# A hybrid decode layer on one core: projection operands in rows of one offset, value products two heads at a time, part of the last residual add on TensorE

## The chip, the cores and the metric

The kernel runs on one core of a Trainium2 chip. The metric is device time of one execution, in microseconds (us). The engines named below are TensorE (PE in the profile; PEld is its weight load), VectorE (DVE), ScalarE (ACT), GpSimd (POOL) and the DMA queues, of which SyncE's (SP) carries most. SBUF is the memory that the engines work from, PSUM the one that PE adds up in.

## The reference

One layer for a prompt of 1024 tokens with 16 learned meta tokens ahead of it, and for 64 sample tokens (8 sequences of 8), all in float32 with a width of 2048:

```python
h = rmsnorm(xp, norm_pre)                       # the same for xs, the sample tokens
q_a, k_a, v_a, gate_a, q_g, k_g, v_g, gate_g, z = split(h @ w_in)
log_f = log_sigmoid(z @ w_a2 + b_a) / 16
att_o = swa_prompt(q_a, k_a, v_a, sinks, rel_bias)   # 16 heads of 64, 4 of keys, window 128
gla_o, s_fin = gla_prompt(q_g, k_g, v_g, log_f)      # 4 heads, a state of 128x256 each
mixed = concat([att_o * silu(gate_a), rmsnorm(gla_o) * silu(gate_g)])
xp = xp + rmsnorm(mixed @ w_out, norm_post)
# samples: swa_sample over cached keys and values, gla_chunk from the cached state
return y_prompt, y_sample, the last 128 keys and values, states (prompt and sample)
```

## The kernel before, in words

Tokens lie along the free axis. Half A is 512 of them (16 meta and 496 of the prompt), half B 592 (528 of the prompt, 64 of the samples). The width of 2048 is 16 K-tiles of 128 partitions. The order of the work is: `in_half(A)`, all input projections of half A; `in_half(B)`, the same for half B; `out_first`, the output projection of half A; and `out_second` twice, the output projection of half B for its token columns 0 to 295 and then 296 to 591 (`last`). The weights come anew from DRAM for each of these passes.

Each float32 product is three matmuls with operands of type float32r (L377): the tokens are kept as two tiles, `hh` (rounded) and `hl` (the rest), which `split` (L192) writes, one pair for each K-tile, 16 of each; a weight block is `whi` (ACT, L341) and `wlo` (DVE, L343), made from `wraw`, 512 KB, which SP loads (L332, three buffers). `proj` (L362) adds up `whi*hh`, `whi*hl` and `wlo*hh` over 16 K-tiles in PSUM tiles `mm`. In half A a matmul has 512 columns, in half B two of 296 stand side by side, in `out_first` there is one of 496, in each pass of `out_second` one of 296. That makes 768 of 512 columns, 2112 of 496 and 5760 of 296, each with 128 rows of weights. So the `hh` and `hl` tiles are read by all 8640 of these matmuls; a tile is `[128, 592]`, 2368 bytes in each partition, and the 32 lie one behind the other in SBUF in the order in which `split` makes them.

Around the projections stand the lanes: generators (`att`, `glas`, `side`) which `proj` advances in its middle and at its end (`mid`, `end`). The scheduler keeps nearly everything in the order of the program text; `pin` makes it do so. Attention of half A and B is `attend` and `kv_tokens`; the decode's attention is `attend_ext` (L602), run twice, once for each pair of key heads: its value products (L674 to L680) multiply probabilities with new and cached values for one head, 64 columns of the array, and then for the other. `gla` (L690) is the gated linear attention.

What goes over from half A to B are the last 128 keys and values of each key pair (`kcar`, `vcar`) and the four states (`scar`), kept in SBUF tiles; POOL copies keys and values there (L493, L494) and back (L475, L1072), and the states are written and read in place (L891).

At the end the last pass has its 16 output tiles in eight slots `os_`; `finish` (L1224) computes the norm's factor `rs` from the sum of squares (a matmul with ones, L1229), multiplies each slot with it (L1248) and adds the residual `x` (L1249), both on DVE, while ACT's queue issues the stores.

Of the kernel before, what the change touches and what calls it, by code (L numbers as in the profile page):

```python
# [7 lines left out]
F32 = mybir.dt.float32  # L8
F32R = mybir.dt.float32r
# [14 lines left out]
TT = (M, M + 80)  # L24
W = max(TT)
FT_BUFS = 14

# [13 lines left out]
class Kernel:  # L41
    def __init__(self, tc, ins, outs, stack):
        self.tc = tc
        self.nc = tc.nc
        self.i = ins
        self.o = outs
        pool = lambda **kw: stack.enter_context(tc.tile_pool(**kw))
        self.const = pool(name="const", bufs=1)
        self.hp = pool(name="hp", bufs=1)
        self.wp = pool(name="wp", bufs=1)  # L50
        self.fp = pool(name="fp", bufs=1)
        self.sp_ = pool(name="sm", bufs=1)
# [35 lines left out]
    def setup_late(self):  # L88
# [11 lines left out]
        self.mix = [[self.dp.tile([P, TT[h]], F32, name=f"mix{h}_{k}") for k in range(KT)] for h in range(2)]  # L100
        self.kcar = c.tile([P, 2, P], F32, name="kcar")
        self.vcar = c.tile([P, 2, P], F32, name="vcar")
        self.scar = c.tile([P, 4, 256], F32, name="scar")
        yield
# [87 lines left out]
    def split(self, src, T, kt, scale=None, c0=0):  # L192

        nc = self.nc
        hi = self.hp.tile([P, W], F32R, name="hh", bufs=KT)
        lo = self.hp.tile([P, W], F32R, name="hl", bufs=KT)
        if scale is None:
            nc.scalar.copy(hi[:, c0:T], src[:, c0:T])
            nc.vector.tensor_tensor(lo[:, c0:T], src[:, c0:T], hi.bitcast(F32)[:, c0:T], ALU.subtract)  # L199
        else:  # L200
            nc.scalar.activation(hi[:, c0:T], src[:, c0:T], AF.Copy, scale=scale)  # L201
            nc.vector.scalar_tensor_tensor(lo[:, c0:T], src[:, c0:T], scale, hi.bitcast(F32)[:, c0:T],  # L202
                                           op0=ALU.mult, op1=ALU.subtract)
        self.hh[kt] = hi
        self.hl[kt] = lo
# [265 lines left out]
    def kv_tokens(self, H, c, kf, vT, vt, kh, kl):  # L471

        nc = self.nc
        if H.i:
            nc.gpsimd.tensor_copy(vt[:, 0, :], self.vcar[:, c, :])  # L475
            ps = self.ps()
            nc.tensor.transpose(ps[:16, :P], vT[:, M:M + 16], self.ident)
            nc.tensor.transpose(ps[:64, P:2 * P], vT[:, M + 16:M + 80], self.ident)
            nc.scalar.copy(vt[:16, 5, :], ps[:16, :P])
            nc.scalar.copy(vt[:64, 6, :], ps[:64, P:2 * P])  # L480
# [11 lines left out]
        if H.i == 0:  # L492
            nc.gpsimd.tensor_copy(self.kcar[:, c, :], kf[:, 512:640])  # L493
            nc.gpsimd.tensor_copy(self.vcar[:, c, :], vt[:, 4, :])  # L494
        else:
# [24 lines left out]
    def attend(self, H, c, g, q, gate, vt, kh, kl):  # L520
# [8 lines left out]
        if H.i == 0:  # L529
            first = self.sm([P, 2, P], "first", 1)  # L530
            nc.vector.tensor_tensor(first, bias, self.neg.unsqueeze(1).to_broadcast([P, 2, P]), ALU.add)
# [70 lines left out]
    def attend_ext(self, c, qx, gx, kf, vt):  # L602
# [66 lines left out]
        po = self.ps()  # L669
        for v in range(2):  # L670
            d = slice(64 * v, 64 * v + 64)
            sb = sbs[:, v]
            for w in range(2):
                nc.tensor.matmul(po[d, w * P:(w + 1) * P], vt[:64, 6, d], sb[:64, 256 + w * P:256 + (w + 1) * P],  # L674
                                 start=True, stop=False)
                for b in range(4):
                    sl = slice(w * P + 32 * b, w * P + 32 * b + 32)
                    nc.tensor.matmul(po[d, sl], vc[w][:, b, d], sb[:, sl], start=False, stop=(b == 3))
            nc.tensor.matmul(po[d, 256:320], vt[:, 4, d], tsb[:, v, :64], start=True, stop=False)
            nc.tensor.matmul(po[d, 256:320], vt[:16, 5, d], tsb[:16, v, 64:], start=False, stop=True)  # L680
        pov = po[:, :256].rearrange("p (b g t) -> p b g t", b=8, g=4)
# [8 lines left out]
    def gla(self, H, hd, zT, io):  # L690
# [174 lines left out]
        nc.vector.tensor_tensor(qe[:, :T], q[:, :T], qe[:, :T], ALU.mult)  # L865

        ktT = self.sm([P, 4, P], "kT", 2)
        ps = self.ps()
# [3 lines left out]
        if H.i:  # L872
# [6 lines left out]
            nc.scalar.copy(ktx[:64, 1], ps[:64, P:2 * P])  # L879
            nc.vector.tensor_tensor(ktx[64:, 1], ps[:64, P:2 * P], ktx.bitcast(F32)[:64, 1], ALU.subtract)  # L880
            st = [self.ft()[:, :512].rearrange("p (b d) -> p b d", b=2) for _ in range(4)]
            for b in range(4):
                self.pin(nc.sync.dma_start(out=st[b], in_=self.i["state"][hd][:, 2 * b:2 * b + 2]))
        yield
        S = [self.scar[:, hd, :] if H.i else None]
        for j in range(4):
# [153 lines left out]
    def in_half(self, H):  # L1040
        nc = self.nc
        kf = vt = kh = kl = qx = gx = None
        for u in range(4):
# [23 lines left out]
            if u % 2 == 0:  # L1067
# [126 lines left out]
    def out_second(self, H, cols, slots, last):  # L1194
# [29 lines left out]
        def finish():  # L1224
# [10 lines left out]
            def load(j):  # L1235
                x = self.ft()
                nc.sync.dma_start(out=two(x), in_=src[:, 2 * j:2 * j + 2, c0:c1])
                return x

            lead = 5 if last else 2  # L1240
            xs = [load(j) for j in range(lead)]
            before = []
            out = nc.scalar if last else nc.sync

            pin = self.pin if last else lambda x: x

            def norm(o, x, k):
                pin(nc.vector.tensor_tensor(o, o, rs[:, :T].unsqueeze(1).to_broadcast([P, k, T]), ALU.mult))  # L1248
                pin(nc.vector.tensor_tensor(o, o, x, ALU.add))  # L1249

            for j in range(KT // 2):
                if before:
                    out.dma_start(**before.pop())
# [3 lines left out]
                if last and j == KT // 2 - 1:  # L1257
                    for k in range(2):
                        norm(o[:, k:k + 1], x[:, k:k + 1], 1)
                        out.dma_start(out=dst[:, 2 * j + k:2 * j + k + 1, c0:c1], in_=o[:, k:k + 1])  # L1260
                    break
                norm(o, x, 2)
                before.append(dict(out=dst[:, 2 * j:2 * j + 2, c0:c1], in_=o))
                if last:
                    out.dma_start(**before.pop())
                yield
            if before:
                out.dma_start(**before.pop())

# [160 lines left out]
```

## Time and profile before

| What | Value |
|---|---|
| Time, median of 3 runs (lowest to highest) | 1728.17 us (1721.74 to 1729.71) |
| The profiled execution: time, span of the trace | 1732.93 us, 1731.2 us |
| Granted TensorE clock, mean of the span | 0.991 |
| PE busy, weight loads busy | 1698.1 us (98%), 1532.8 us (89%) |
| DVE, ACT, POOL busy | 1061.2, 740.8, 19.8 us |
| DMA | 213.71 MB, mean 123 GB/s |

The profile is of one execution, the trace of which is read below. A matmul's recorded duration is from its start to its modelled end and is longer than the step to the next one's start, since they are pipelined; what a matmul costs in a row of them is the step. A group's row gives the count behind an x, then the busy time of all and the mean of one.

### The profile page before, as it was taken

How to read it: one execution, taken by the hardware profiler on the slowest of the kernel's cores; microseconds unless marked ns; L12 is line 12 of the kernel's file. 1: busy time of each engine (PE TensorE's matmuls, PEld its weight loads, DVE VectorE, ACT ScalarE, POOL GpSimd, SP SyncE). 2: the span in 40 equal slices, each digit the busy share in tenths (PEclk: the TensorE clock that was granted, in tenths of full speed). 3: DMA queues.
4: the chain of work that ended last, by engine and by line, in shares of the span. 5: the costliest groups of instructions: out<-in, count | busy, mean ns of one | idle time of the engine just before them, and what ended most of it. 6: DMA issues, size and time to landing. Idle time of an engine off the chain costs nothing.

```text
span 1731.2 us, 30015 instructions
## 1 busy us (share of the span) xinstructions
PE 1698.1 (98%) x11836; PEld 1532.8 (89%) x11836; DVE 1061.2 (61%) x2360; ACT 740.8 (43%) x1606; POOL 19.8 (1%) x60
## 2 busy tenths in 40 slices
PE   8999999999999999999999999999999999999995
PEld 6778888888888999999999999999997788899995
DVE  6485686675756757545665566465857433675655
ACT  6354355443434535342444243343435333644442
POOL 0000000000000000000000000000000000000000
PEclk9999999999999999999999999999999999999998
DMA  6743433222234422323222232223325333686664
GB/s 232 125 129 98 134 109 117 91 87 93 94 96 157 167 83 71 103 71 97 83 81 91 94 113 65 92 84 101 97 83 192 107 98 98 235 273 210 217 208 162
DMA packets 85742, 213.71 MB, mean 123 GB/s; under 512 B 11504, under 2 KB 33936, under 8 KB 85568
## 3 DMA queue, kind: packets, MB, share of 16 engines
q1 hardware_dynamic: 82416, 204.90, 36.1%
q0 software_dynamic: 992, 4.46, 1.7%
q10 hardware_dynamic: 2192, 2.43, 0.4%
q8 instruction: 93, 1.52, 0.4%
q14 instruction: 49, 0.40, 0.1%
HBM read 186.32 MB, written 27.39 MB: 123 GB/s over the span
## 4 chain that ended last, share of the span: by engine, by line
PE 89%; DMA 5%; DVE 3%; ACT 1%; issue 1%; SPq 0%; DVEq 0%; ACTq 0%
PE mm L377 76%; PE ps L551 2%; DMA wraw<-in_win 1%; PE ps L581 1%; DMA ft<-in_xB 1%; PE ps L403 1%; PE ps L567 1%; PE ps L890 1%; PE ps L918 1%; DVE wlo L343 1%; PE ps L920 1%; DMA st<-in_xA 1%; PE ps L583 1%; PE ps L797 1%; DMA ft<-in_xA 1%
## 5 line engine op out<-in xcount | busy, mean ns | idle before, releaser
L377 PE MATMUL mm<-hh,whi 128*128 128x296 f32 (+2 forms) x2880 | 845.7, 333 | 7.0 <-ACT whi L341 5.9
L377 PE MATMUL mm<-hh,wlo 128*128 128x296 f32 (+2 forms) x2880 | 839.4, 331 | 3.8 <-DVE wlo L343 3.7
L377 PE MATMUL mm<-hl,whi 128*128 128x296 f32 (+2 forms) x2880 | 838.1, 330 | 0.3 <-DVE hl L199 0.3
L341 ACT CAST whi<-wraw 128x512 fp32r<-128x512 f32 x544 | 334.5, 619 | 777.9 <-PE mm L377 703.3
L343 DVE TENSOR_TENSOR wlo<-wraw,whi 128x512 fp32r<-128x512 f32 x544 | 369.9, 687 | 400.7 <-ACT whi L341 376.4
L377 PEld LDWEIGHTS mm<-hh,whi 128*128 128x128 f32 x2880 | 506.2, 189 | 49.7 <-ACT whi L341 6.6
L377 PEld LDWEIGHTS mm<-hh,wlo 128*128 128x128 f32 x2880 | 507.2, 189 | 44.3 <-DVE wlo L343 6.5
L377 PEld LDWEIGHTS mm<-hl,whi 128*128 128x128 f32 x2880 | 508.9, 189 | 37.6 <-issue 0.9
L431 DVE TENSOR_TENSOR ft<-mm,rs 128x592 f32<-128x592 f32 (+2 forms) x59 | 42.9, 727 | 64.4 <-PE mm L377 64.3
L515 ACT ACTIVATE st<-st,nm 128x128 f32<-128x128 f32 (+1 forms) x140 | 54.7, 392 | 51.7 <-DVE nm L509 51.6
L570 DVE TENSOR_TENSOR pT<-ps,c_sides 128x512 f32<-128x512 f32 x64 | 41.5, 682 | 0.9 <-PE ps L567 0.8
L433 DVE SCALAR_TENSOR_TENSOR ft<-mm,rs 128x592 f32<-128x592 f32 (+1 forms) x23 | 16.7, 725 | 32.2 <-PE mm L377 32.0
L764 DVE TENSOR_TENSOR ft<-ft 128x512 f32<-128x512 f32 (+2 forms) x48 | 33.3, 703 | 0.2
L812 DVE COPY_PREDICATED A<-masks,ps 32x64 f32<-32x64 uint8 x128 | 30.9, 241 | 3.0 <-PE ps L801 0.7
L551 PE MATMUL ps<-kh,qst 128*128 128x256 f32 x128 | 32.7, 290 | 0.0
L538 ACT CAST qst<-ft 64x256 fp32r<-64x256 f32 x64 | 25.9, 404 | 15.5 <-PE ps L551 12.5
L551 PE MATMUL ps<-kl,qst 128*128 128x256 f32 x128 | 31.1, 278 | 0.0
L765 ACT ACTIVATE ft<-ft 128x256 f32<-128x256 f32 (+2 forms) x48 | 20.3, 423 | 19.8 <-DVE ft L764 19.7
L539 DVE TENSOR_TENSOR qst<-ft,qst 64x256 fp32r<-64x256 f32 x64 | 26.9, 420 | 3.1 <-ACT qst L538 1.2
L202 DVE SCALAR_TENSOR_TENSOR hl<-ft,wpre,hh 128x512 fp32r<-128x512 f32 (+1 forms) x32 | 24.1, 788 | 6.7 <-ACT hh L201 6.7
L581 PE MATMUL ps<-pT,vt 128*64 128x128 f32 x256 | 27.3, 291 | 0.8 <-DVE pT L570 0.8
L555 DVE CUSTOM_DVE_ANT_0 st<-ps,bias 128x128 f32<-128x128 f32 x112 | 26.7, 283 | 0.0
(332 smaller groups left out, 1456.7 us busy)
## 6 DMA issues: line engine op xcount, KB each, us to landing
wraw<-in_win SPq DMA_DIRECT2D x174, 512.0 KB, 3.9
wraw<-in_wout SPq DMA_DIRECT2D x96, 512.0 KB, 4.0
ft<-in_xB SPq DMA_DIRECT2D x48, 296.0 KB, 4.6
ft<-mix SPq DMA_DIRECT2D x16, 296.0 KB, 5.9
ft<-in_xA SPq DMA_DIRECT2D x16, 256.0 KB, 5.8
ft<-in_state SPq DMA_DIRECT2D x16, 256.0 KB, 5.6
out_gs<-ft SPq DMA_DIRECT2D x16, 256.0 KB, 2.3
mix<-ft SPq DMA_DIRECT2D x16, 248.0 KB, 2.0
```

Of the source, the lines that this page charges most:

```text
L341: nc.scalar.copy(hi, r)
L343: nc.vector.tensor_tensor(lo, r, hi.bitcast(F32), ALU.subtract)
L377: nc.tensor.matmul(ps[:, j, :p1 - p0], w[:, k % 4, :], h[kt][:, p0:p1], start=(kt == 0 and a == 0), stop=(kt == KT - 1 and a == 2))
L431: self.nc.vector.tensor_tensor(o, src, r, ALU.mult)
L515: nc.scalar.activation(s, s, AF.Exp, bias=nm[:R, j:j + 1], accum_out=den[:R, j:j + 1])
L539: nc.vector.tensor_tensor(qs[o, v], qd, qs.bitcast(F32)[d, v], ALU.subtract)
L551: nc.tensor.matmul(ps[:, t], qs[:, v, t * P:t * P + P], k[:, v, k0:k0 + 256], start=(j == 0), stop=(j == 1))
L555: nc.vector.tensor_tensor_reduce(out=st[:, v, t], in0=ps[:, t, P:], in1=b[:, v], scale=1.0, scalar=NEG, op0=ALU.add, op1=ALU.max, accum_ou ...
L570: nc.vector.tensor_tensor(sb[:, j], pt, self.sides[:, j:j + 1].to_broadcast([P, 4, P]), ALU.mult)
L581: nc.tensor.matmul(pov, vt[:, j + 1, d], sb[:, 1, 2 * v + t], start=True, stop=alone)
L764: nc.vector.tensor_tensor(ev, bv, bv[:, :, h - 1:h].to_broadcast([P, ns, 2 * h]), ALU.subtract)
L812: nc.vector.copy_predicated(A[r, :, r].rearrange("p j (s e) -> p j s e", e=2 * h)[:, :, :, h:], mk[r, 16 * b:16 * b + 16].rearrange("p (s ...
```

## The change

There are four edits. **One**: the 32 token tiles are 640 floats wide instead of 592, 2560 bytes, and their pool is allocated first. Columns used stay the same. In each partition they began at byte 31296 before, with row after row 2368 bytes further; read as an offset within 512 bytes, the rows began at 64, 256, 448, 128, 320, 0, 192, 384 and again from 64, in the order in which the tiles are made, that is hh and hl of one K-tile and then of the next. Now the first begins at byte 16512 and all 32 at 128 within 512. **Two**: `kcar`, `vcar` and `scar` are DRAM tiles; eight stores and eight loads from SP's queue take the place of POOL's copies, the state gets a fifth buffer `S`, and `first` in `attend` takes a slot of `kx`. **Three**: in `attend_ext` the value products alternate between the two heads, with one more `yield` in between. **Four**: in the last pass, slots 0, 1, 2 and 5 get their residual added on PE, by matmuls with the identity into PSUM, and ACT copies the sum out and issues the store; slots 3, 4, 6 and 7 stay on DVE, and SP issues their stores.

```diff
+WH = 640
...
+        self.hp = pool(name="hp", bufs=1)
         self.const = pool(name="const", bufs=1)
-        self.hp = pool(name="hp", bufs=1)
...
-        self.kcar = c.tile([P, 2, P], F32, name="kcar")
-        self.vcar = c.tile([P, 2, P], F32, name="vcar")
-        self.scar = c.tile([P, 4, 256], F32, name="scar")
+        self.kcar = [self.dp.tile([P, P], F32, name=f"kcar{j}") for j in range(2)]
+        self.vcar = [self.dp.tile([P, P], F32, name=f"vcar{j}") for j in range(2)]
+        self.scar = [self.dp.tile([P, 256], F32, name=f"scar{j}") for j in range(4)]
...
-        hi = self.hp.tile([P, W], F32R, name="hh", bufs=KT)
-        lo = self.hp.tile([P, W], F32R, name="hl", bufs=KT)
+        hi = self.hp.tile([P, WH], F32R, name="hh", bufs=KT)
+        lo = self.hp.tile([P, WH], F32R, name="hl", bufs=KT)
...
-            nc.gpsimd.tensor_copy(vt[:, 0, :], self.vcar[:, c, :])
+            nc.sync.dma_start(out=vt[:, 0, :], in_=self.vcar[c])
...
-            nc.gpsimd.tensor_copy(self.kcar[:, c, :], kf[:, 512:640])
-            nc.gpsimd.tensor_copy(self.vcar[:, c, :], vt[:, 4, :])
+            nc.sync.dma_start(out=self.kcar[c], in_=kf[:, 512:640])
+            nc.sync.dma_start(out=self.vcar[c], in_=vt[:, 4, :])
...
-        for v in range(2):
-            d = slice(64 * v, 64 * v + 64)
-            sb = sbs[:, v]
-            for w in range(2):
-                nc.tensor.matmul(po[d, w * P:(w + 1) * P], vt[:64, 6, d], sb[:64, 256 + w * P:256 + (w + 1) * P],
+        heads = [(v, slice(64 * v, 64 * v + 64)) for v in range(2)]
+        for w in range(2):
+            for v, d in heads:
+                nc.tensor.matmul(po[d, w * P:(w + 1) * P], vt[:64, 6, d], sbs[:64, v, 256 + w * P:256 + (w + 1) * P],
                                  start=True, stop=False)
-                for b in range(4):
-                    sl = slice(w * P + 32 * b, w * P + 32 * b + 32)
-                    nc.tensor.matmul(po[d, sl], vc[w][:, b, d], sb[:, sl], start=False, stop=(b == 3))
+            for b in range(4):
+                sl = slice(w * P + 32 * b, w * P + 32 * b + 32)
+                for v, d in heads:
+                    nc.tensor.matmul(po[d, sl], vc[w][:, b, d], sbs[:, v, sl], start=False, stop=(b == 3))
+            if w == 0:
+                yield
...
+            S0 = self.sm([P, 256], "S", 5)
+            nc.sync.dma_start(out=S0, in_=self.scar[hd])
...
-            S.append(self.scar[:, hd, :] if j == 3 and H.i == 0 else self.sm([P, 256], "S", 4))
+            S.append(self.sm([P, 256], "S", 5))
...
-        if H.i:
+        if H.i == 0:
+            nc.sync.dma_start(out=self.scar[hd], in_=S[4])
+        else:
...
-                    nc.gpsimd.tensor_copy(kf[:, 0:128], self.kcar[:, c, :])
+                    nc.sync.dma_start(out=kf[:, 0:128], in_=self.kcar[c])
...
+            def add(j, t, start):
+                for k in range(2):
+                    pin(nc.tensor.matmul(room[j][k], self.ident, t[:, k], start=start, stop=not start))
...
+            for j in range(3):
+                tokens(j)
...
+                if j in (0, 1, 2, 5):
+                    pin(scale(o, 2))
+                    add(j, o, False)
+                    if j == 1:
+                        for k in range(2):
+                            pin(nc.scalar.copy(o[:, k], room[j][k]))
+                    else:
+                        pin(nc.scalar.copy(o, room[j, 0]))
+                    nc.scalar.dma_start(out=to, in_=o)
+                    if j == 2:
+                        tokens(5)
+                elif j < KT // 2 - 1:
+                    pin(scale(o, 2))
+                    pin(nc.vector.tensor_tensor(o, o, x, ALU.add))
+                    nc.sync.dma_start(out=to, in_=o)
```

`tokens(j)` takes a PSUM tile for slot j and puts the residual there by `add(j, x, True)`.

The three places where the order of instructions differs follow, each with the rows before and then the rows now. The first is PE's row of the first `attend_ext`, from the first value product (out<-in, with `pT` probabilities, `vt` new values, `ft` cached values).

```order
L674 MATMUL ps<-pT,vt 64x128
L678 MATMUL ps<-pT,ft 64x32 x4
L674 MATMUL ps<-pT,vt 64x128
L678 MATMUL ps<-pT,ft 64x32 x4
L679 MATMUL ps<-ft,vt 64x64
L680 MATMUL ps<-ft,vt 64x64
L674 MATMUL ps<-pT,vt 64x128
L678 MATMUL ps<-pT,ft 64x32 x4
L674 MATMUL ps<-pT,vt 64x128
L678 MATMUL ps<-pT,ft 64x32 x4
L679 MATMUL ps<-ft,vt 64x64
L680 MATMUL ps<-ft,vt 64x64
```

Now the same place reads:

```order
L677 MATMUL ps<-pT,vt 64x128
L190 MATMUL ps<-ft,ones_r 128x512 x2
L677 MATMUL ps<-pT,vt 64x128
L682 MATMUL ps<-pT,ft 64x32 x8
L677 MATMUL ps<-pT,vt 64x128 x2
L682 MATMUL ps<-pT,ft 64x32 x8
L686 MATMUL ps<-ft,vt 64x64 x2
L688 MATMUL ps<-ft,vt 64x64 x2
```

Before, a head's products stand together and only the second head's follow; now the heads alternate in each x8 and x2, and the new `yield` puts two 512-column sums of another lane (L190) behind the first product.

The second place is DVE's row at the end of the kernel, the last pass's `finish` (names are those of the slots; L1248 and now L1254 multiply, L1249 and now L1312, L1317 add).

```order
L1248 TENSOR_TENSOR kl<-kl,rs 128x592
L1249 TENSOR_TENSOR kl<-kl,ft 128x592
L1248 TENSOR_TENSOR zT<-zT,rs 128x592
L1249 TENSOR_TENSOR zT<-zT,ft 128x592
L1248 TENSOR_TENSOR vg<-vg,rs 128x592
L1249 TENSOR_TENSOR vg<-vg,ft 128x592
L1248 TENSOR_TENSOR vg<-vg,rs 128x592
L1249 TENSOR_TENSOR vg<-vg,ft 128x592
L1248 TENSOR_TENSOR ft<-ft,rs 128x592
L1249 TENSOR_TENSOR ft<-ft 128x592
L1248 TENSOR_TENSOR ft<-ft,rs 128x592
L1249 TENSOR_TENSOR ft<-ft 128x592
```

Now:

```order
L1254 TENSOR_TENSOR kl<-kl,rs 128x592
L1254 TENSOR_TENSOR zT<-zT,rs 128x592
L1254 TENSOR_TENSOR vg<-vg,rs 128x592 x2
L1312 TENSOR_TENSOR vg<-vg,ft 128x592
L1254 TENSOR_TENSOR ft<-ft,rs 128x592
L1312 TENSOR_TENSOR ft<-ft 128x592
L1254 TENSOR_TENSOR ft<-ft,rs 128x592 x2
L1312 TENSOR_TENSOR ft<-ft 128x592
L1254 TENSOR_TENSOR ft<-ft,rs 128x296
L1317 TENSOR_TENSOR ft<-ft 128x296
L1254 TENSOR_TENSOR ft<-ft,rs 128x296
L1317 TENSOR_TENSOR ft<-ft 128x296
```

Both pieces have the first slot's multiplication in their first row; the piece of before stops two slots short of its end, the piece of now reaches it. Eight multiplications and additions alternated; now four of the additions are gone from DVE.

The third place is SP's row about the second key pair's `kf` in half B (`out_kp` and `out_ks` are outputs).

```order
L332 DMA wraw<-in_win 128x1024
L496 DMA out_kp<-kf 128x128
L499 DMA out_ks<-kf 128x64
L332 DMA wraw<-in_win 128x1024
L687 DMA mix_0_438<-gx 128x80
```

Now:

```order
L335 DMA wraw<-in_win 128x1024
L1085 DMA kf<-kcar_455 128x128
L499 DMA out_kp<-kf 128x128
L502 DMA out_ks<-kf 128x64
L335 DMA wraw<-in_win 128x1024
L695 DMA mix_0_438<-gx 128x80
```

A load of the carried keys now stands in SP's row behind a weight load and ahead of the next one.

## Rows read from the trace of the kernel before

**Rows 1.** The page: busy time by engine; the chain that ended last, by line
```profile
PE 1698.1 (98%) x11836; PEld 1532.8 (89%) x11836; DVE 1061.2 (61%) x2360; ACT 740.8 (43%) x1606; POOL 19.8 (1%) x60
...
PE mm L377 76%; PE ps L551 2%; DMA wraw<-in_win 1%; PE ps L581 1%; DMA ft<-in_xB 1%; PE ps L403 1%; PE ps L567 1%; PE ps L890 1%; PE ps L918 1%; DVE wlo L343 1%; PE ps L920 1%; DMA st<-in_xA 1%; PE ps L583 1%; PE ps L797 1%; DMA ft<-in_xA 1%
```

**Rows 2.** Groups of PE by form: count | busy us, mean ns | idle before, releaser
```profile
L377 PE MATMUL mm<-hh,whi 128*128 128x496 f32 x704 | 277.6, 395 | 6.8 <-ACT whi L341 5.9 <-ACT hh L201 0.8
```

**Rows 3.** PE in time, first output pass, 496 columns: start us, duration us, line, op
```profile
1380.13 0.39 PE L377 MATMUL mm<-hl,whi 128*128 128x496 f32 x1
...
1411.80 0.38 PE L377 MATMUL mm<-hl,whi 128*128 128x496 f32 x1
1412.02 0.38 PE L377 MATMUL mm<-hh,wlo 128*128 128x496 f32 x1
...
1413.81 0.39 PE L377 MATMUL mm<-hl,whi 128*128 128x496 f32 x1
1414.04 0.39 PE L377 MATMUL mm<-hh,wlo 128*128 128x496 f32 x1
...
1474.86 0.39 PE L377 MATMUL mm<-hh,whi 128*128 128x496 f32 x1
```

**Rows 4.** The same, 512 columns (half A) and twice 296 (half B), first and last
```profile
51.35 0.39 PE L377 MATMUL mm<-hh,whi 128*128 128x512 f32 x1
...
496.72 0.39 PE L377 MATMUL mm<-hl,whi 128*128 128x512 f32 x1
...
701.09 0.44 PE L377 MATMUL mm<-hh,whi 128*128 128x296 f32 x2
...
1289.27 0.43 PE L377 MATMUL mm<-hh,wlo 128*128 128x296 f32 x2
```

**Rows 5.** PE in time: attention values of half A, then the first decode value products
```profile
635.54 0.45 PE L581 MATMUL ps<-pT,vt 128*64 128x128 f32 x4
...
636.03 0.44 PE L581 MATMUL ps<-pT,vt 128*64 128x128 f32 x4
...
1046.60 0.43 PE L674 MATMUL ps<-pT,vt 64*64 64x128 f32 x2
1046.96 0.65 PE L678 MATMUL ps<-pT,ft 128*64 128x32 f32 x8
...
1048.88 0.43 PE L674 MATMUL ps<-pT,vt 64*64 64x128 f32 x2
...
1051.77 0.80 PE L187 MATMUL ps<-ft,ones_r 128*128 128x512 f32 x1
```

**Rows 6.** Stretches: us, busy us (count) of PE, PEld, DVE, ACT, POOL, PEclk
```profile
1050.30:1057.10 6.80, 6.80 (x60) 5.65 (x61) 3.60 (x14) 0.00 (x0) 0.29 (x1) 0.50 0.13 36
1367.80:1374.50 6.70, 6.70 (x25) 5.47 (x26) 1.33 (x6) 0.24 (x1) 0.00 (x0) 0.50 0.34 101
1715.90:1731.20 15.30, 0.00 (x0) 0.00 (x0) 12.11 (x19) 0.00 (x0) 0.00 (x0) 0.50 0.45 160
```

**Rows 7.** All engines in time, the end of the kernel
```profile
1712.06 1.43 PE L1229 MATMUL ps<-ft,ones 128*128 128x296 f32 x4
...
1716.05 0.77 DVE L1248 TENSOR_TENSOR kl<-kl,rs 128x592 f32<-128x592 f32 x1
1716.86 0.77 DVE L1249 TENSOR_TENSOR kl<-kl,ft 128x592 f32<-128x592 f32 x1
1717.55 0.77 DVE L1248 TENSOR_TENSOR zT<-zT,rs 128x592 f32<-128x592 f32 x1
...
1727.89 0.47 DVE L1249 TENSOR_TENSOR ft<-ft 128x296 f32<-128x296 f32 x1
```

**Rows 8.** DMA issues by line: count, KB each, median us to landing
```profile
wraw<-in_win SPq DMA_DIRECT2D x174, 512.0 KB, 3.9
...
bias<-R SPq DMA_DIRECT2D x16, 128.0 KB, 2.2
```

**Rows 9.** Waits of the SP queue: us in total, times, longest us
```profile
SPq L332 <- DVE wlo L343: 1025.4, 221, 15.4
```

More of the change, by code (lines that the diff above doesn't have):

```diff
@@ L529, in attend @@
         if H.i == 0:
-            first = self.sm([P, 2, P], "first", 1)
+            first = self.sm([P, 2, P], "kx", 1, F32R).bitcast(F32)
             nc.vector.tensor_tensor(first, bias, self.neg.unsqueeze(1).to_broadcast([P, 2, P]), ALU.add)
@@ L669, in attend_ext @@
         po = self.ps()
-        for v in range(2):
-            d = slice(64 * v, 64 * v + 64)
-            sb = sbs[:, v]
-            for w in range(2):
-                nc.tensor.matmul(po[d, w * P:(w + 1) * P], vt[:64, 6, d], sb[:64, 256 + w * P:256 + (w + 1) * P],
-                                 start=True, stop=False)
-                for b in range(4):
-                    sl = slice(w * P + 32 * b, w * P + 32 * b + 32)
-                    nc.tensor.matmul(po[d, sl], vc[w][:, b, d], sb[:, sl], start=False, stop=(b == 3))
+        heads = [(v, slice(64 * v, 64 * v + 64)) for v in range(2)]
+        for w in range(2):
+            for v, d in heads:
+                nc.tensor.matmul(po[d, w * P:(w + 1) * P], vt[:64, 6, d], sbs[:64, v, 256 + w * P:256 + (w + 1) * P],
+                                 start=True, stop=False)
+            for b in range(4):
[4 more added lines that the diff above has]
+                yield
+        for v, d in heads:
             nc.tensor.matmul(po[d, 256:320], vt[:, 4, d], tsb[:, v, :64], start=True, stop=False)
+        for v, d in heads:
             nc.tensor.matmul(po[d, 256:320], vt[:16, 5, d], tsb[:16, v, 64:], start=False, stop=True)
@@ L865, in gla @@
         nc.vector.tensor_tensor(qe[:, :T], q[:, :T], qe[:, :T], ALU.mult)
+        S0 = None
         ktT = self.sm([P, 4, P], "kT", 2)
@@ L884, in gla @@
         yield
-        S = [self.scar[:, hd, :] if H.i else None]
+        S = [S0]
         for j in range(4):
@@ L1238, in load, with scale @@
                 return x
+            def scale(o, k):
+                return nc.vector.tensor_tensor(o, o, rs[:, :T].unsqueeze(1).to_broadcast([P, k, T]), ALU.mult)
             lead = 5 if last else 2
             xs = [load(j) for j in range(lead)]
+            if last:
+                finish_last(rs, xs, load, two, dst, scale)
+                return
             before = []
[L1243 to L1249, printed above, removed]
             for j in range(KT // 2):
                 if before:
-                    out.dma_start(**before.pop())
+                    nc.sync.dma_start(**before.pop())
                 if j + lead < KT // 2:
@@ L1256, in finish @@
                 o, x = two(os_[j]), two(xs[j])
-                if last and j == KT // 2 - 1:
-                    for k in range(2):
[L1259 to L1265, printed above, removed]
@@ L1266, in finish, with finish_last, tokens @@
-                yield
-            if before:
-                out.dma_start(**before.pop())
+                scale(o, 2)
+                nc.vector.tensor_tensor(o, o, x, ALU.add)
+                before.append(dict(out=dst[:, 2 * j:2 * j + 2, c0:c1], in_=o))
+                yield
+            nc.sync.dma_start(**before.pop())
+        def finish_last(rs, xs, load, two, dst, scale):
+            pin = self.pin
+            room = {}
+            def add(j, t, start):
+                for k in range(2):
+                    pin(nc.tensor.matmul(room[j][k], self.ident, t[:, k], start=start, stop=not start))
+            def tokens(j):
+                if j == 1:
+                    room[j] = [self.ps()[:, :T] for _ in range(2)]
+                else:
+                    m = self.mm()
+                    room[j] = [m[:, k, :T] for k in range(2)]
+                    room[j, 0] = m[:, :, :T]
+                add(j, two(xs[j]), True)
+            for j in range(3):
+                tokens(j)
+            for j in range(len(xs), KT // 2):
+                xs.append(load(j))
+            for j in range(KT // 2):
+                o, x = two(os_[j]), two(xs[j])
+                to = dst[:, 2 * j:2 * j + 2, c0:c1]
+                if j in (0, 1, 2, 5):
+                    pin(scale(o, 2))
+                    add(j, o, False)
+                    if j == 1:
+                        for k in range(2):
+                            pin(nc.scalar.copy(o[:, k], room[j][k]))
+                    else:
+                        pin(nc.scalar.copy(o, room[j, 0]))
[6 more added lines that the diff above has]
+                    nc.sync.dma_start(out=to, in_=o)
+                else:
+                    for k in range(2):
+                        pin(scale(o[:, k:k + 1], 1))
+                        pin(nc.vector.tensor_tensor(o[:, k:k + 1], o[:, k:k + 1], x[:, k:k + 1], ALU.add))
+                        nc.sync.dma_start(out=to[:, k:k + 1], in_=o[:, k:k + 1])
```

## Prediction

> **What bounds the kernel now.** I read the page first: PE is busy in 98% of the span, and in the chain of work that ended last the projection's matmul alone, L377, holds 76% [rows 1]. So only what shortens PE's steps, takes work from PE, or shortens the stretches at the two ends without PE can count. Next the groups of PE by form: of the nine groups of L377's 8640 products the one that waits most waits 6.8 us in all [rows 2], so there is no wait worth removing: the operands come in time. The weights have slack too: a block lands 3.9 us after its issue [rows 8], and SP waits 1025.4 us of the span for VectorE's `wlo` to free a buffer [rows 9]: it runs ahead, held by room alone. A DMA more in that queue, or a us less of VectorE, therefore reaches PE only after that lead is gone.
>
> What is left is the step from one product's start to the next. I took it from the trace in time, where the products stand back to back. In the first output pass 423 steps between the first and last row of [rows 3] have a mean of 224.5 ns at 496 columns. By the same working it is 231.6 ns at 512 columns (647 steps) and 136.6 ns at 296 (3285 steps), in the stretches that [rows 4] mark. At 2.4 GHz and a column per cycle 496 columns would be 207 ns, 296 would be 123, so each step holds some 13 to 18 ns beyond its columns. All steps of L377 are 2112 x 0.2245 + 768 x 0.2316 + 5760 x 0.1366 = 474.1 + 177.9 + 786.8 = 1439 us. One per cent of a step is 14 us.
>
> Steps are not equal: [rows 3] have one of 0.22 us (1411.80 to 1412.02) and one of 0.23 (1413.81 to 1414.04), and the order of long and short ones comes again every four K-tiles to a ns or two. I sorted them by where the token row that is read begins within 256 bytes. At 496 columns rows at 64, 0, 192 and 128 have means of 225.3, 223.4, 226.7 and 222.6 ns (105 to 107 steps each); at 512 columns 232.8, 233.0, 230.5 and 230.1; at 296 in half B 136.3, 136.8, 137.2 and 135.9. The rows at 128 are shortest each time. But this doesn't prove that the offset does it: rows at 128 are only `hl` tiles of odd K-tiles, and the weight's place in its tile has the period of four as well.
>
> **The change part by part.**
>
> *Rows of one offset.* No instruction goes or comes. If every step takes what rows at 128 take now, the gains are 2112 x (224.5 - 222.6) = 4.0 us, 768 x (231.6 - 230.1) = 1.2 us and 5760 x (136.6 - 135.9) = 4.0 us: 9.2 us less. The bounds: with every 496-column step at the 0.22 us of [rows 3] (2112 x 4.5 ns = 9.5 us less, about double), the 296-column steps gaining double as well (8.0) and 1.2 as above, 19 us less; with every step at the slowest of the four means (226.7, 233.0, 137.2) 4.6 + 1.1 + 3.5 = 9 us more. I take 9.2 less, since the sign is the same in all three shapes.
>
> [Rows 3] show 224.5 ns for 496 columns with a spread by position. The Trainium skill, "TensorE: Matmul & The Clock Gate", section "Back-to-back issue gap", gives the warm gap of an isolated matmul by its columns alone, N/2.4 + 2.5 ns, with no word for where the operand lies; the trace agrees with neither the size (an estimate from it is 209 ns) nor the equality of steps.
>
> *Value products.* Before, the products of a group pair stand from 1046.60 to 1051.77, 5.2 us [rows 5]: twice 2.28 us at full speed (1046.60 to 1048.88) and the rest at half. The second time they come with one product of L377 between. The x8 of L678 take 0.65 us of records with 32 columns each, 0.06 to 0.08 us a product for 13 ns of columns, and the x2 of L674, 128 columns, 0.36 us to the next, 0.18 each. Where the two heads' halves of the array already alternate, in `attend` of half A, eight products of 128 columns stand from 635.54 to 636.03 [rows 5], 0.06 each, a third of that. With heads alternating, 64 columns and the other 64, I let two thirds of a head's 2.28 us go, 1.5 us each time, 3 us in all. Bounds: nothing, and 2 x 2.28 = 4.6 us if one head is wholly hidden behind the other.
>
> [Rows 5] show products that alternate between column halves at a third of the time. The Trainium skill, "TensorE: Matmul & The Clock Gate", section "Part 3: Packing small matmuls", says that a weight load overlaps with matmuls in flight only where the row group differs, and both heads here read the same rows; by it this term is nothing and the sum 3 us higher.
>
> *Cold stretches.* The granted clock was 0.50 in 1050.3 to 1057.1 and in 1367.8 to 1374.5 [rows 6], 6.8 and 6.7 us. Both times PE had been at those narrow products for about 4 us before. What is done at half speed in 6.75 us takes half of that at full: 3.4 us lost each, 6.8 in all. Now a group pair is some 3.6 us at full speed, cut by two sums of 512 columns in the first place and by products of L377 in the second. I take 5 us less; the bounds are 0 and 6.8.
>
> *The end.* In [rows 7] the factor `rs` is ready at 1716.05, VectorE multiplies and adds slot after slot (an addition starts 0.81 us after its multiplication's start, the next multiplication 0.69 after that), and its last instruction ends at 1728.36; the span ends 2.85 us later with the last store. Four additions leave VectorE: 4 x 0.7 = 2.8 us off. What is late next is PE's and ScalarE's path for slot 5, whose factor is multiplied about sixth, some 6 us after `rs`: two identity products at the half speed of [rows 6] (from 1715.9), about 1 us by half of the four records in 1.43 us of L1229, doubled for the clock, one copy of 592 columns (0.77 us, what VectorE takes for as many) and a store. That is through before VectorE's last. The residuals go into PSUM earlier, while VectorE works out `rs`. I take 2.5 us less; bounds 3.2 less and, if the identity products take 2 us a slot and the stores follow them, 1.3 less.
>
> *Carries.* Eight stores and eight loads of 64 or 128 KB join SP. The nearest row is a load of 128 KB, 2.2 us to landing [rows 8]. A load of keys waits for its buffer in SP's row ahead of a weight load; the store of the same keys' tile, which stood in that place before, waited for the projection itself, which is later. So no weight is held up longer than before, and the lead of [rows 9] covers 2 us. The keys come some 2 us later than by POOL; VectorE may stand for that, and PE not. I take 0; bounds 0 and 3 us more, one landing that PE waits for in each of the two pairs with part of it hidden.
>
> Sum, against the profiled execution's own 1732.9 us: 9.2 + 3 + 5 + 2.5 = 19.7 less, 1713. That execution is 4.8 us above the median of the runs shown; the runs lie 8 us apart, the size of a few cold stretches, and of these the change takes some. So I set the time a little lower than the sum: 1712 us.
>
> **The rivals.** *The offset does nothing.* The sorted means then come from the operand's kind and the weight's place. For it: rows at 128 are one kind only, and the other three classes change places from shape to shape. Against it: the lowest class is the same in three shapes. Time: 1732.9 - 10.5 = 1722 us.
>
> *The heads don't overlap, and the cold stretches stay.* For it: the x8 of L678 are already at 0.06 to 0.08 us, as close as `attend`'s alternating ones. Against it: the 0.18 us of L674 beside the 0.06 of L581, equal in columns. Time: 1732.9 - 9.2 - 2.5 = 1721 us.
>
> *Rows lock into the short step.* If steps differ because offsets change from row to row, one offset may give the short one throughout: 19 less in place of 9.2, 1703 to 1704 us.
>
> *Rows lock into the long step* (the slower side). Whatever makes a step long at some offsets may, with all 32 tiles at one offset, hold at every one. With the 0.23 of [rows 3] in place of 0.2245 everywhere, 2.4% of 1439 us is 35 us more: 1722 + 35 = 1757 us. It decides from 1.7 ns a step on (14.6 us over 8640 steps, which eat the other gains of 10.5 and reach the slower side of the limit below). For it: the mix of offsets averages now, and an average goes if all are alike. Against it: the mean at 128 is no longer than any other.
>
> **How the numbers follow.** What a measurement can tell from no change is about 0.5%, 8.6 us: faster is below 1719.5, slower above 1736.8. The forecast has a chance of 0.45 (its own range 1705 to 1719), the offset that does nothing 0.27, heads and clock as before 0.10, the short step 0.08, the long step 0.10. Faster: 0.45, 0.08 and, since 1721 and 1722 stand near the limit, 0.08 of the two in the middle, 0.61. Slower is the long step alone, 0.10. Same: the rest, 0.29. The range of 8 in 10 goes from 1701, below the short step, to 1728, above the two in the middle with the carries' 3 us; the long step is left out.
>
> **What would show it.** Steps in time: the 496-column step near 222.6 ns, 512 near 230, 296 near 135.9, and no difference between K-tiles. If they are 224.5, 231.6 and 136.6, the offset does nothing; 228 or more is the long step. In the stretches: no granted clock of 0.50 about the two value products, and a group pair below 4 us. At the end: from `rs` to the end of the span 12 to 13 us where 15.2 are now. In the waits: SP still held by `wlo`, and PE's idle before `whi` and `wlo` no longer than now; if the 6.8 us of [rows 2] grow by more than 3 us, the carries' loads are in the weights' way, and the prediction is wrong in what it costs at nothing.

## The result, and the profile after

The changed kernel takes 1714.9 us (median of 4 runs, 1714.07 to 1716.37) where before takes 1728.2; the ratio is 0.9931, 95% interval 0.9905 to 0.9957. It is faster by 13.3 us, and inside the forecast's range (1712, 1701 to 1728). On another chip, beside experiments, it was 0.9913 (0.9898 to 0.9929). Against the profiled execution of before (1732.93 us) its own, 1715.20, is 17.7 us shorter. One profiled execution below, that of the first experiment, was disturbed and its trace is not read.

The page of the changed kernel shows the same bound as [rows 1]: PE busy 7.8 us less, idle 10 us less.

```profile
PE 1690.3 (99%) x11868; PEld 1525.1 (89%) x11868; DVE 1058.1 (62%) x2356; ACT 744.3 (43%) x1611; POOL 16.5 (1%) x52
...
PE mm L380 77%; PE ps L554 2%; DMA ft<-in_xB 1%; DMA wraw<-in_win 1%; PE ps L584 1%; PE ps L406 1%; PE ps L570 1%; PE ps L901 1%; PE ps L931 1%; DVE wlo L346 1%; PE ps L933 1%; DMA st<-in_xA 1%; PE ps L586 1%; PE ps L805 1%; DMA ft<-in_xA 1%
```

The value products of the first pair [rows 5], in time on PE (start, duration; L677 the new values, L682 the cached ones, L686 and L688 the samples' extra columns):

```profile
1044.27 0.43 PE L677 MATMUL ps<-pT,vt 64*64 64x128 f32 x2
1044.63 0.73 PE L190 MATMUL ps<-ft,ones_r 128*128 128x512 f32 x2
1045.29 0.43 PE L677 MATMUL ps<-pT,vt 64*64 64x128 f32 x2
1045.65 0.66 PE L682 MATMUL ps<-pT,ft 128*64 128x32 f32 x16
1046.24 0.43 PE L677 MATMUL ps<-pT,vt 64*64 64x128 f32 x4
1046.60 0.66 PE L682 MATMUL ps<-pT,ft 128*64 128x32 f32 x16
1047.09 0.32 PE L686 MATMUL ps<-ft,vt 128*64 128x64 f32 x4
1047.33 0.33 PE L688 MATMUL ps<-ft,vt 16*64 16x64 f32 x4
```

Sixteen records of L682 now stand in 0.66 us, where eight stood in 0.65: two heads share each step. The products take 0.36 us ahead of the cut (1044.27 to 1044.63) and some 2.25 from 1045.29 on, 2.6 where two heads took 4.56 at full speed, so 2.0 less; no stretch at half clock follows. The clock by stretch, which was 0.50 in all three of [rows 6] (the columns are theirs):

```profile
1035.00:1045.00 10.00, 10.00 (x123) 8.38 (x122) 6.74 (x39) 5.61 (x25) 0.00 (x0) 1.00 0.20 66
1045.00:1055.00 10.00, 10.00 (x130) 8.77 (x129) 8.51 (x24) 3.46 (x8) 0.00 (x0) 1.00 0.30 87
1353.00:1363.00 10.00, 10.00 (x85) 7.42 (x84) 5.07 (x19) 4.94 (x16) 0.00 (x0) 1.00 0.42 117
1700.00:1713.40 13.40, 6.64 (x25) 4.17 (x23) 9.53 (x16) 2.67 (x5) 0.00 (x0) 0.89 0.57 199
```

It is 1.00 about both products. At the end the mean is 0.89: the clock falls to 0.50 only at 1710.5, behind the identity products, which PE now has to do there.

The trace of before has one more stretch at half clock, in half B (790.9 to 794.3 us, shown in the last section); about that place the changed kernel's trace gains 2.7 of the 17.7 us, which none of the four parts of the forecast covers.

The end [rows 7], all engines:

```profile
1696.70 1.43 PE L1242 MATMUL ps<-ft,ones 128*128 128x296 f32 x4
...
1700.69 0.78 DVE L1254 TENSOR_TENSOR kl<-kl,rs 128x592 f32<-128x592 f32 x1
1701.39 0.77 DVE L1254 TENSOR_TENSOR zT<-zT,rs 128x592 f32<-128x592 f32 x1
...
1706.57 1.26 PE L1281 MATMUL mm<-ft,ident 128*128 128x296 f32 x4 [0.79 <-DVE ft L1254]
...
1707.87 0.65 ACT L1306 COPY ft<-mm 128x592 f32<-128x592 f32 x1 [2.03 <-PE mm L1281]
...
1708.92 1.26 SPq L1318 DMA_DIRECT2D out_yB<-ft  x2
1709.30 0.47 DVE L1317 TENSOR_TENSOR ft<-ft 128x296 f32<-128x296 f32 x1
```

From `rs` (1700.69, the start of the first multiplication) to the span's end at 1713.4 it is 12.7 us where 15.15 were [rows 7]: 2.45 less. VectorE itself ends 3.2 us sooner after `rs` (9.08 us against 12.31); the last store takes 0.8 of that back.

Where the page has a landing for the carried tiles, it comes 1.6 to 5.1 us after the issue (it has none for the loads of keys and states), and SP's wait for room is nearly what it was [rows 8, 9] (DMA issues: KB, median us to landing; then waits of SP: us, times, longest):

```profile
wraw<-in_win SPq DMA_DIRECT2D x174, 512.0 KB, 3.9
...
scar<-S SPq DMA_DIRECT2D x4, 128.0 KB, 1.7
...
kcar<-kf SPq DMA_DIRECT2D x2, 64.0 KB, 2.8
vcar<-vt SPq DMA_DIRECT2D x2, 64.0 KB, 1.6
...
vt<-vcar SPq DMA_DIRECT2D x2, 64.0 KB, 5.1
```

```profile
SPq L335 <- DVE wlo L346: 986.6, 217, 15.3
```

PE's waits for `whi` and `wlo` are 10.5 us in all against 9.6; in the group of [rows 2] the idle time is 8.3 us against 6.8.

### The profile page after: what moved, and what is told of

Read it like the earlier page. It is cut to its first block, busy times and chain, and to the rows that moved or that the text cites. A ratio compares the mean times of both kernels' runs of the same rounds, so it can differ in the third digit from the quotient of the medians.

```text
span 1713.4 us, 30094 instructions
## 1 busy us (share of the span) xinstructions
PE 1690.3 (99%) x11868; PEld 1525.1 (89%) x11868; DVE 1058.1 (62%) x2356; ACT 744.3 (43%) x1611; POOL 16.5 (1%) x52
## 4 chain that ended last, share of the span: by engine, by line
PE 90%; DMA 5%; DVE 3%; ACT 1%; issue 1%; SPq 0%; DVEq 0%; ACTq 0%
PE mm L380 77%; PE ps L554 2%; DMA ft<-in_xB 1%; DMA wraw<-in_win 1%; PE ps L584 1%; PE ps L406 1%; PE ps L570 1%; PE ps L901 1%; PE ps L931 1%; DVE wlo L346 1%; PE ps L933 1%; DMA st<-in_xA 1%; PE ps L586 1%; PE ps L805 1%; DMA ft<-in_xA 1%
## 5 line engine op out<-in xcount | busy, mean ns | idle before, releaser
L541 ACT CAST qst<-ft 64x256 fp32r<-64x256 f32 x64 | 25.9, 404 | 17.2 <-PE ps L554 13.3
```

## The experiments

Steps below are means from one start to the next where products of one form stand back to back, from each trace (636 steps at 512 columns, some 1063, 3838, 615 and twice 631 in the other columns):

| Kernel | 512, half A | 496, half A | 296, half B | 496, first output pass | 296, pass 1 | 296, last pass |
|---|---|---|---|---|---|---|
| before | 231.8 | 224.7 | 136.6 | 224.7 | 136.7 | 136.7 |
| changed | 229.1 | 225.9 | 136.1 | 224.0 | 133.4 | 136.5 |
| e4 rows and carries only | 229.1 | 226.0 | 136.2 | 224.0 | 133.5 | 136.9 |
| e9 rows of 2368 bytes | 231.8 | 225.1 | 136.5 | 224.6 | 136.3 | 136.9 |
| e6 all at 0 | 229.1 | 226.0 | 136.2 | 224.4 | 133.6 | 137.2 |
| e7 all at 64 | 229.1 | 226.0 | 136.2 | 224.4 | 133.4 | 136.4 |
| e10 all at 160 | 229.0 | 225.8 | 136.1 | 224.0 | 133.6 | 137.1 |
| e11 second part at 1280 | 229.0 | 225.7 | 133.5 | 224.0 | 133.1 | 133.5 |

The theory at the outset: of the gain some 5 us come from the steps, 8 from the value products, 2.5 from the end, and nothing from or to the carries. The rival: the offset does nothing, and the executions differ by the clock alone. Ratios are against before on the same chip, 95% intervals behind them. The changed kernel itself ran beside e5 to e8 only, so e1 to e4 and e9 to e12 are set against it across chips, and differences of 1 to 3 us in medians are no more than hints.

**One part undone.** Each is the changed kernel with one edit taken back: e1 `WH = W`, e2 the old loop over heads, e3 the old `finish`.

> The changed kernel with its token rows 592 floats wide again (2368 bytes), so that their offsets vary; all else as changed. Theory (rows of one offset are worth what the steps of the two traces differ by, some 5 us): about 1720 us, and the 296-column step of pass 1 goes back from 133.4 to about 136.7 ns. Rival (the offset does nothing, the steps differ by chance of the two executions): 1715 us, steps as in the changed kernel.

> The changed kernel with the value products of attend_ext in the order of before, one head after the other, and without the extra yield. Theory (order is worth the overlap and the two stretches at half clock, some 9 us together by the stages of the traces): about 1723 to 1724 us, with the granted clock at 0.50 behind both value products. Rival (the clock fell there by chance): about 1717 us, a clock of 1.00 and only the 2 to 3 us of overlap lost.

> The changed kernel with the end of before: all residual adds on VectorE, stores from ScalarE's queue. Theory (four additions of 0.7 us leave the last chain): about 1717.4 us, 2.5 more. Rival (the stores, not VectorE, set the end): within 1 us of the changed kernel's 1714.9.

Measured: e1 1718.25 us, 0.9936 (0.9921 to 0.9952); e2 1723.25, 0.9966 (0.9953 to 0.9979); e3 1716.61, 0.9934 (0.9919 to 0.9949). So the products are the largest part, some 8 us by the medians, as the theory had it (e2's runs go from 1719.4 to 1727.8), and the clock falls again with the old order (e2, columns as above):

```profile
1049.00:1054.00 5.00, 5.00 (x48) 3.85 (x48) 2.76 (x11) 0.00 (x0) 0.00 (x0) 0.50 0.51 150
1366.00:1372.00 6.00, 6.00 (x24) 4.69 (x24) 1.33 (x6) 0.00 (x0) 0.00 (x0) 0.50 0.38 111
```

The end is worth 1.3 to 1.7 us by the medians, with intervals that overlap, and 2.45 by the rows above. The traces are clear on it: from the start of the last projection product to the end of the span it is 19.2 us in all four kernels with the old end (before, e3, e4, e12) and 16.8 or 16.9 in all nine with the new one. For the rows e1 says 3.4 us by the medians, with intervals that overlap; it was repeated as e9 for its steps.

**Rows and carries alone.** The changed kernel with the old loop and the old `finish`; the carries alone are that with `WH = W`.

> Only the rows of 2560 bytes and the carries through DRAM; value products and end as before. Theory (rows 5 us, carries nothing): about 1723 us against 1728 before, and the clock still at 0.50 behind the value products. Rival 1 (the offset does nothing): 1728. Rival 2 (the carries cost 3 us that the rows win back): 1728 too, with SP or PE waiting at the carried keys or states.

> The carries through DRAM alone: rows of 2368 bytes, value products and end as before; the token pool is first. Theory (the carries cost nothing on PE): within 1.5 us of the kernel before, PE's waits as before. Rival (their loads stand in the weights' way): 2 to 4 us more than the kernel before, with longer waits of PE for whi or wlo in half B.

Measured: e4 1726.61, 0.9998 (0.9986 to 1.001); e12 1727.76, 0.9993 (0.9979 to 1.0007). The carries cost nothing that can be measured (the interval of e12 allows 1.2 us), and PE waits no longer for `wlo` and `whi` (7.6 us against 9.6). In time e4 missed the theory's 1723: it shows no gain, and its interval leaves room for 2.4 us, though its steps are those of the changed kernel and 5 us shorter in sum. Part of this is on record. Its 12 runs have granted clocks of 0.992 and 0.993, where 8 of the 20 of before that ran beside it have 0.994 to 0.996; with the time lost to the clock taken out of each run, as an estimate from these rounded clocks, e4 is some 2 us ahead.

Steps are not time, besides. From the first product of pass 1 to the last of the last pass there are 214.0 (e9), 214.0 (e12) and 216.2 us (before) with rows of 2368 bytes, and 212.0 to 215.1 in the nine traces with rows of 2560 and the second part at 1184: 0.7 less in the mean, where the steps alone give 2.2 to 2.7. In the same two passes PE waits for `wlo` (us, times, longest; before, e9, e12, changed):

```profile
PE mm L377 <- DVE wlo L343: 2.9, 4, 1.6
...
PE mm L380 <- DVE wlo L346: 1.2, 1, 1.2
...
PE mm L380 <- DVE wlo L346: 0.7, 2, 0.4
...
PE mm L380 <- DVE wlo L346: 3.1, 3, 1.6
```

In the nine traces it is 1.0 to 3.2 us, 2.5 in the mean. So part of what shorter steps give there seems to come back as waits for the next block of weights; with before itself at 2.9 this isn't shown, only that the time doesn't follow the steps. The rows' worth lies between e4's 2 us and e9's 5 (below), and the sum of the steps is above both.

**Which offset.** The rows' pool gets an unused tile first, here of 384 bytes:

```diff
         self.hp = pool(name="hp", bufs=1)
+        self.hp.tile([P, 96], F32, name="gap")
```

> The changed kernel as it is, beside the kernel before and the others of this group on one chip. All theories: 1714 to 1717 us; it is the yardstick for the three others.

> The changed kernel with all 32 token rows 384 bytes further, so that they begin at 0 within 512 instead of 128. Theory 1 (the offset itself decides, and 128 is a good one): the 296-column step of pass 1, 133.4 ns in the changed kernel, goes to about 136.3, the 512-column step from 229.1 to about 232, the 496-column step of the first output pass from 224.0 to some 223 to 225; in all about 4 to 6 us more, 1719 to 1721 us. Theory 2 (that the rows are alike is what counts, at whatever offset): the steps stay, 133.4, 229.1 and 224.0 ns, and the time is that of the changed kernel.

> The changed kernel with all 32 token rows 448 bytes further, at 64 within 512. Theory 1 (the offset itself decides): the 296-column step of pass 1 at about 136.8 ns, the 512-column step at about 233, and the 496-column step, whose columns begin 64 bytes into the row and so at 128 now, at about 225; 1720 us. Theory 2 (alike rows are what counts): steps and time of the changed kernel.

Measured: the changed kernel 1715.34, 0.9913 (0.9898 to 0.9929); e6 1714.31, 0.9912 (0.9895 to 0.9929); e7 1713.67, 0.9903 (0.9888 to 0.9919). Time and steps stay: it isn't the offset in memory. But the gap moves everything allocated behind the rows as well, the weight tiles too, so rows and weights kept their distance; whether that distance counts, these three runs can't tell.

> Once more the changed kernel with rows of 2368 bytes, for its steps. Theory (that the rows are alike is what counts): the steps of the kernel before come back, 231.8 ns at 512 columns, 224.7 at 496, 136.6 at 296 in half B and 136.7 in both passes of the second output projection, and the time is 3 to 5 us above the changed kernel's. Rival (the order of the pools, which moved the rows' base, made the steps): the changed kernel's steps, 229.1, 226.0, 136.15 and 133.4 ns, though the rows vary.

> The changed kernel with all rows 32 bytes further, at 160 within 512. In the changed kernel pass 1 reads from a multiple of 64 bytes (133.4 ns a step) and the last pass, 1184 bytes into the row, from 32 beside one (136.6 ns). Theory (a read that begins at a multiple of 64 is quicker once rows are alike): the two change places, 136.6 ns in pass 1 and 133.4 in the last pass; the time about the same, 512 columns slower. Rival (what is around the passes makes the difference, not the offset): 133.4 and 136.6 stay as they are.

Measured: e9 1719.7, 0.9942 (0.9926 to 0.9958); e10 1714.26, 0.9914 (0.9899 to 0.9929). In time e9 is 5.4 us above e10, which ran on the same chip and has the changed kernel's steps; their runs don't overlap (1715.9 to 1720.7 and 1712.7 to 1715.5). In e9 the steps of before are back to within 0.4 ns, so the width of a row makes them and the pools' order does not. Two rows of e9's trace, 47 steps apart, in pass 1 and then in the last pass (start, duration):

```profile
1521.24 0.30 PE L380 MATMUL mm<-hh,whi 128*128 128x296 f32 x1
...
1527.65 0.30 PE L380 MATMUL mm<-hh,wlo 128*128 128x296 f32 x1
...
1628.04 0.30 PE L380 MATMUL mm<-hh,whi 128*128 128x296 f32 x1
...
1634.46 0.30 PE L380 MATMUL mm<-hh,wlo 128*128 128x296 f32 x1
```

6.41 / 47 = 136.4 ns and 6.42 / 47 = 136.6 ns. The same products in the changed kernel, and at the start of its last pass:

```profile
1519.38 0.30 PE L380 MATMUL mm<-hh,whi 128*128 128x296 f32 x1
...
1525.65 0.29 PE L380 MATMUL mm<-hh,wlo 128*128 128x296 f32 x1
...
1597.10 0.30 PE L380 MATMUL mm<-hh,whi 128*128 128x296 f32 x1
...
1603.36 0.30 PE L380 MATMUL mm<-hh,wlo 128*128 128x296 f32 x1
...
1626.85 0.30 PE L380 MATMUL mm<-hh,whi 128*128 128x296 f32 x1
...
1633.30 0.30 PE L380 MATMUL mm<-hh,wlo 128*128 128x296 f32 x1
```

6.27 / 47 = 133.4 ns in pass 1, 6.26 / 47 = 133.2 early in the last pass, and 6.45 / 47 = 137.2 later in it: in the last pass with alike rows a step sits at one of two levels. In this trace the first 144 products of the pass have the short one, up to two sums of another line (L1242), and those behind them the long one. e5 is the same program, and the same two products, 48 and 95 places into the last pass, stand there like this:

```profile
1595.56 0.30 PE L380 MATMUL mm<-hh,whi 128*128 128x296 f32 x1
...
1601.99 0.30 PE L380 MATMUL mm<-hh,wlo 128*128 128x296 f32 x1
```

That is 6.43 / 47 = 136.8 ns with every address as before, so no address alone sets the level. The table's means for this pass mix the two. In e10 pass 1 stays at 133.6 although it reads from 32 beside a multiple of 64, and the last pass at 137.1 although it reads from a multiple: my theory of multiples of 64 in memory fell.

**Where the second part begins.** Part two of half B goes to column 320 of its row, 1280 bytes in, instead of 296:

```diff
+GAP = WH // 2 - W // 2
...
+            two = lambda t, n: t[:, :2 * n].rearrange("p (j n) -> p j n", j=2)[:, :, :T // 2]
+            vs, vh, vl = two(src, T // 2), two(hi, WH // 2), two(lo, WH // 2)
...
-                            nc.tensor.matmul(ps[:, j, :p1 - p0], w[:, k % 4, :], h[kt][:, p0:p1],
+                            nc.tensor.matmul(ps[:, j, :p1 - p0], w[:, k % 4, :], h[kt][:, p0 + GAP * (p0 > META):p1 + GAP * (p0 > META)],
...
```

`split` writes with these views, and the products of `zstep` read with the same shift.

> The changed kernel with the second 296 columns of half B stored 320 floats into the row instead of 296, 1280 bytes, so that both parts begin at a multiple of 64 bytes. Theory (multiple of 64 is quicker once rows are alike): the last pass goes to 133.4 ns a step, 768 x 3.2 = 2.5 us, and half B from 136.15 towards 133.4, 4224 x up to 2.7 ns = up to 11 us; 1702 to 1712 us. Rival (the offset within the row does nothing): steps and time of the changed kernel, 1715 us.

Measured: 1703.05 us, 0.9856 (0.9836 to 0.9875), the fastest of all: some 25 us below before, and 11.2 below e10 on the same chip. Products 46 steps apart in half B (x2: both parts), then 47 apart in the last pass:

```profile
595.03 0.43 PE L386 MATMUL mm<-hh,whi 128*128 128x296 f32 x2
...
601.16 0.43 PE L386 MATMUL mm<-hh,wlo 128*128 128x296 f32 x2
...
1615.82 0.30 PE L386 MATMUL mm<-hh,whi 128*128 128x296 f32 x1
...
1622.09 0.29 PE L386 MATMUL mm<-hh,wlo 128*128 128x296 f32 x1
```

6.13 / 46 = 133.3 ns in half B and 6.27 / 47 = 133.4 in the last pass. By the table 4224 x 2.6 ns = 11.0 us and 768 x 3.0 = 2.3 us, 13.3 in sum, against 12.5 between the spans of the two traces (1713.4 and 1700.9). PE's instructions and their order are those of the changed kernel. So where the second part lies in its row does count. e10 excludes that it is its place in memory modulo 64. The distance to the weight tile that is read with it would fit the passes as a whole (a multiple of 64 bytes in pass 1 everywhere, e10 included, and in e11's last pass; 32 beside one in the other last passes), but by itself it is not enough: the last pass has both levels at one distance, and in the changed kernel's half B the products of the first part, at a multiple of 64, take 136.5 ns and those of the second, 32 beside one, 135.8. No run changed that distance alone. The cause stays open.

**Without the cut.** The changed kernel without the two lines `if w == 0: yield`.

> The changed kernel with the heads' value products alternating but without the extra yield between them, so that all stand in one place without other work between. Theory (overlap of the two heads' halves shortens the stretch enough that the clock stays): within 1.5 us of the changed kernel, no granted clock of 0.50 there. Rival (it is the cut by the yield that keeps the clock): a stretch at 0.50 behind the value products again, 3.4 us each where it comes, up to 7 us more.

Measured: 1715.08, 0.9912 (0.9897 to 0.9927), the clock 1.00 about both products:

```profile
1036.00:1050.00 14.00, 14.00 (x208) 11.31 (x194) 10.70 (x53) 7.81 (x28) 0.00 (x0) 1.00 0.28 84
1345.00:1362.00 17.00, 17.00 (x187) 12.92 (x186) 9.75 (x48) 7.55 (x28) 0.00 (x0) 1.00 0.38 116
```

The alternating order alone keeps the clock; the cut adds nothing that shows. Whether it does so because the products are over sooner or because both halves of the array work at once, no run separates.

## Why the prediction was right, point by point

*Rows of one offset*, 9.2 us: the direction was right and the term mis-sized. The steps give 768 x 2.7 = 2.1 us at 512 columns (1.2 forecast), 4224 x 0.5 + 768 x 3.3 + 768 x 0.2 = 4.8 us at 296 (4.0), and at 496 columns, where 4.0 were forecast, 768 x 0.7 - 1344 x 1.2 = 1.1 us lost; 5.8 in sum. In time it is less, 3.4 us by e1, 5.4 by e9 and e10, some 2 by e4: the forecast took every ns of a step for time, and in the last two passes the time didn't follow.

The step that failed is the one from the sorting to alike rows: that a class of rows keeps its step when all rows are of that class. At 512 columns and in pass 1, where a read begins at the row's start, the step came out at the short class's and below it (229.1 for 230.1, 133.4 for 135.9). The 496-column products of half A and of the first output pass all begin 64 bytes into the row, and one went up and the other down; in half B the first part begins at the row's start and has 136.5. So where a read begins doesn't explain it either, and what makes a step long stays open.

The confusion was also described wrongly. In the program of before the 16 `hh` tiles lie first and the 16 `hl` tiles behind them (from byte 69184 on), so `hh` and `hl` of one K-tile begin at the same offset, and rows at 128 within 256 bytes are both tiles of every fourth K-tile, not `hl` tiles alone. The prediction's own counts say so: four classes of 105 to 107 out of 423 steps, where `hl` tiles of odd K-tiles would be one product in six. What could stand behind the classes was the K-tile and its weight's place, not the operand's kind. The rival that the offset does nothing is refuted by e9 for the pitch, and right for the place in memory (e6, e7, e10). That the sign came out as forecast owes something to luck.

*Value products and cold stretches*, 3 + 5 = 8 us: e2 puts 8.3 us on them. The two stretches of [rows 6] at these products are gone, with and without the cut (e8). In the stages of the traces of before and after, the first products account for 4.7 us and the second for 5.0; some 2.0 of each are the overlap (4.56 to 2.6 us), the rest is the clock. The rule that the prediction quotes from the Trainium skill ("TensorE: Matmul & The Clock Gate", "Part 3: Packing small matmuls"), and from which it reads that this gains nothing since both heads read the same rows, did not decide here: sixteen records stand in the 0.66 us where eight stood in 0.65.

*The end*, 2.5 us: 2.45 by the rows, 2.3 or 2.4 by all thirteen traces, 1.3 to 1.7 by e3's medians; that VectorE would stay last was right, while the stores' 0.8 us were not in the sum. The identity products were doubled for the clock, and ran at 1.00.

*Carries*, 0: e12 confirms it, with at most 1.2 us of cost in its interval.

*The base.* The sum came to 1713 and I went to 1712 for the median; the terms as measured, 2 to 5.4 for the rows, 8.3 for the products and 2.4 for the end, make 13 to 16, where the medians first shown have 13.3 and e5 15.8. The forecast's 9.2 for the rows was some 4 us too much or more, and 1712 lies 2.9 us from 1714.9 with some luck: the errors were small beside the spread of before, whose runs lie 10 us apart (1723.70 to 1733.78) where those of the changed kernel lie 4 us apart (1712.84 to 1716.76).

The long step, the slower rival, appeared in part: in the 496 columns of half A (225.9 ns against 224.7, the 1344 x 1.2 = 1.6 us above) and in most of the last pass (137.2 against 136.7, under 1 us).

## What to carry to other kernels

Where PE is busy all the time, measure its step from start to start, by stage and by where each read begins; 3 ns in 136 were worth 11 us here (e11), and no wait in the profile shows them. Before sorting by an address, take the address that the instruction reads, not that of its tile, and vary one distance at a time: a gap in front of a pool moves all that lies behind it. Narrow products that alternate between halves of the array stand beside one another and keep the clock at its upper level; this was worth some 8 us here for a change of order alone.

## What was not expected

With rows of equal pitch a 296-column step has two levels, 133.3 and 137.2 ns, and goes over from one to the other within a pass (at 1610 us in the changed kernel, behind two sums of L1242; in e5, the same program, the pass has the long level from its start); with rows of 2368 bytes it is a mean of 136.6 of mixed steps. And the half-clock stretches are not of the kernel alone: in before's profiled execution the clock also fell at 790.9 us, behind a wait of PE of 2.04 us for VectorE in another lane; the changed kernel and the carries alone show none there, nor does any other trace read. All those kernels have the carries through DRAM, so one trace of before can't tell whether the change or that execution made the difference. How much of the span is at half clock does change from execution to execution: the runs of before have granted clocks from 0.991 to 0.996, and with them its wider spread. The three stretches, of before, the changed kernel and the carries alone (columns as in [rows 6]):

```profile
790.90:794.30 3.40, 3.40 (x16) 3.40 (x15) 2.26 (x7) 0.62 (x1) 0.00 (x0) 0.50 0.71 216
```

```profile
787.00:796.00 9.00, 8.13 (x65) 7.71 (x65) 6.32 (x21) 3.72 (x12) 0.00 (x0) 1.00 0.52 165
```

```profile
787.00:800.00 13.00, 12.13 (x97) 11.54 (x96) 8.12 (x18) 3.58 (x13) 0.00 (x0) 1.00 0.50 153
```
